# A four-layer token-mixing backbone on one core: two-tensor additions, copies and scale-and-add forms change engines, and the order inside the three-product matmul

## The chip, the cores and the metric

One NeuronCore of one Trainium2 chip runs the whole program in one launch. The metric is the device time in microseconds (us) from the first to the last instruction of one execution, as the runtime reports it, and the median over runs. The engines are called PE (TensorE, the matrix engine), DVE (VectorE), ACT (ScalarE), POOL (GpSimd) and SP (SyncE, which issues the DMAs here).

## The reference, cut to what matters

Four layers work on 512 tokens (256 context, then 256 latent) of width 1024. Each layer has a token mixer and a SwiGLU channel mixer, both with adaLN modulation and RMS norms before and after.

```python
hg, rw, gt = split(modulate(rms_norm(x)) @ w_in)  # 2560 + 1920 + 2048 columns
o_hg = hgrn2_branch(hg)    # 4 heads, both directions: gated linear recurrence, S = diag(f) S + k v^T
o_rw = rwkv7_branch(rw)    # 8 heads, both directions: S = S diag(w) + (S a) b^T + v k^T, o = S r
m = sigmoid(gt_a) * (o_hg @ proj_a) + sigmoid(gt_b) * (o_rw @ proj_b)
x = x + gate * rms_norm(m @ w_out)
x = x + gate * rms_norm((silu(h @ w1a) * (h @ w1b)) @ w2)  # hidden width 2816
```

The first three layers carry context and latent tokens through everything. In the last layer only the latent tokens are needed after the recurrences.

## The kernel before, in words

Activations lie with channels on the partitions and the 512 tokens along the free axis. All large products are done in three parts: a weight tile is loaded as float32 (`wr`, 256 KB: four blocks of 128x128), ACT rounds it to `wh` (fp32r), and a subtraction writes the remainder `wl = wr - wh`; the activations are split likewise into `hh` and `hl`. `mm3` (lines 494 to 497) then accumulates three matmuls per 128x128 block into one PSUM tile `p_ps`. `proj` (line 521) makes one 128-row output of such a product from `load_split` (line 477) and `mm3`. There are four raw buffers and three each for `wh` and `wl`. Which engine makes `wl` is set by `LO` (line 62): DVE in the mixers, POOL in the rest of the first three layers, either in the rest of the last layer.

A layer (line 744) has two stages. **The mixer** runs these streams, which the program lists at line 1312 and which overlap freely:

- `rw_pair` (line 812), four times: prepares two RWKV heads (projections, decays, `kd` at line 888, masked score products `SC`, copies into `SC` at line 951).
- `rw_solve` (line 985), four times: a triangular solve on DVE, 30 steps of two dependent small operations (`S<-XS`, `XS<-XS,S` in the trace), then small matmuls.
- `rw_chain` (line 1031), four times: eight chunk steps, each a handful of 64x64 matmuls (`c_ps`), ACT copies, POOL's `S0P = S * pcs` and DVE's updates of `UV` and `S`; at the end the group norm with its scale and shift at line 1130.
- `hg_head` (line 1140), four times: projections, then seven levels. A level exponentiates the cumulated sums `HA` and `HB` on ACT into `X` and `Y` (`hX` and `hY` in the trace), multiplies `X` by `q` on DVE, makes scores on PE, and doubles the sums' reach with one addition into `HB` and one into `HA` (lines 1232 to 1234, on POOL).
- `gate_tiles` (line 1300): the sixteen gate projections, which nothing in the mixer waits for.

**The rest of a layer** (from line 1343 on) is `proj_a`, `proj_b`, `w_out`, the norms and the channel mixer, with the modulation vectors of the next layer made on DVE beside it.

No queue order is written by hand. Every operation is recorded as a node (`Plan.add`, line 150) with a cost in ns (`Plan.cost`, line 198), and a list scheduler (line 243) puts the nodes of each engine into one fixed order before the program is emitted; nodes recorded through `plan.any` go to DVE or POOL, whichever the plan has free first. Each engine then runs its own list in order and waits on semaphores. The lines of the cost function that bear on the edits are these (`n` is elements per partition; the last three are POOL's, of which the very last serves two-tensor operations and copies):

```python
if eng == "act":
    return (51.0 if psum else 93.0) + n * 0.833 + 93.0 * bool(ptr)
if eng == "vec":
    two = name in ("tensor_scalar", "tensor_copy") and not psum
    return 67.0 + n * (0.53 if two else 1.042) + 61.0 * ptr
...
if name == "tensor_scalar":
    if ptr:
        return 686.0
...
return 150.0 + 2.1 * n
```

Because every instruction is emitted from one place, all carry line 343 in the trace; the tiles tell them apart. In the trace `X8a` holds `TA` (so `kd` is `X8a<-X8a,vv,der`), `X4c` holds `TC`, `BK` the split of a sum's input in `psum2` (line 503), and `nacc<-SS` is the copy at line 1231.

Of the kernel before, what the change touches and what calls it, by code (L numbers as in the profile page):

```python
# [9 lines left out]
F32 = mybir.dt.float32  # L10
F32R = mybir.dt.float32r
U8 = mybir.dt.uint8
AF = mybir.ActivationFunctionType
ALU = mybir.AluOpType
# [15 lines left out]
C = 64  # L30
# [323 lines left out]
def body(ctx, tc, xT, cc, ada_w, w_in, rw_lo, rw_g2, proj_a, proj_b, w_out, ffn_w1, ffn_w2,  # L354
         vecs, lbl, c_id, c_bo, c_sc, c_hg, c_sh, out, depth=4):
    nc = tc.nc
    plan = Plan(nc, tc)
# [134 lines left out]
        return hi, lo  # L492

    def mm3(ps, wh, wl, xh, xl, first, last):
        pe.matmul(ps, wh, xh, start=first, stop=False)
        pe.matmul(ps, wh, xl, start=False, stop=False)
        pe.matmul(ps, wl, xh, start=False, stop=last)

    def split_to(hi, lo, src):
        act.activation(hi, src, AF.Copy)  # L500
# [2 lines left out]
    def psum2(w, src, hi, lo, rg=slice(0, T), tag="s"):  # L503

        act.activation(hi[:, rg], src[:, rg], AF.Copy)
        plan.any.tensor_tensor(out=lo[:, rg], in0=src[:, rg], in1=hi[:, rg].bitcast(F32), op=ALU.subtract)
        ps = sps(tag)
        pe.matmul(ps[:, rg], w, hi[:, rg], start=True, stop=False)
        pe.matmul(ps[:, rg], w, lo[:, rg], start=False, stop=True)
        return ps  # L510
# [233 lines left out]
    def layer(l, pm, xs, xd, hh, hl):  # L744
        last = l == depth - 1
# [5 lines left out]
        def v1(base, i):  # L751
            return vv[:, base + i:base + i + 1]
# [24 lines left out]
        def stacked(src, tags):  # L777

            xs = [st(t, [P, T], F32R) for t in tags]
            for d, x in enumerate(xs):  # L780
                h, o = hd[d], hd[1 - d]
                act.activation(x[h], src[h], AF.Copy)
                plan.any.tensor_tensor(out=x[o], in0=src[h], in1=x[h].bitcast(F32), op=ALU.subtract)
            return xs

        wd = shifted(rwt(12), 12, lmu, 0, "vt")
# [25 lines left out]
        def rw_pair(p):  # L812
# [29 lines left out]
            pool.tensor_scalar(out=sq, in0=sq, scalar1=2.0 ** -40, scalar2=None, op0=ALU.max)  # L842
            act.activation(sq2, sq2, AF.Ln)
            act.activation(sq, sq, AF.Ln)
            pool.tensor_tensor(out=sq, in0=sq, in1=sq2, op=ALU.add)
            act.activation(sq, sq, AF.Exp, scale=-0.5)
            nkk = TC[:, 0, :]
            vec.scalar_tensor_tensor(out=nkk, in0=k, scalar=der[:, p:p + 1], in1=sq, op0=ALU.mult, op1=ALU.mult)
# [6 lines left out]
            share[p] = (ARt, pcs)  # L855
            lws = [t.rearrange("p (x c) -> p x c", x=4) for t in parts()]
            act.activation(lws[0], lw, AF.Copy)
            plan.any.tensor_tensor(out=lws[1], in0=lw, in1=lws[0].bitcast(F32), op=ALU.subtract)
            KD, BKs = [], []

            def lora(x, d, xs):
# [5 lines left out]
            for d in range(2):  # L867
                rv = rev if d else sec
                rv4 = rev4 if d else fwd4
                psw = lora(0, d, wd)  # L870
                sw = TA[:, 0, :]
                sigm(sec(sw), rv(psw), der[:, 12 + d * 4 + p:13 + d * 4 + p], sw)
                yield 2
                psa_ = lora(1, d, ad)
                if d:
                    TD = st("BK", [P, 2, T])
                a = TA[:, 1, :]
                sigm(sec(a), rv(psa_), der[:, 20 + d * 4 + p:21 + d * 4 + p], a)
                yield 3
                cs = TC[:, 1, :]  # L880
                vec.tensor_tensor_scan(out=cs, data0=rmk, data1=sw, initial=0.0, op0=ALU.mult, op1=ALU.add)
                pool.memset(ep[:, :, 0:1], 1.0)
                csc = cs.rearrange("p (c j) -> p c j", j=C)
                act.activation(ep[:, :, 1:], csc, AF.Exp, scale=-EC)
                ip = sw
                act.activation(ip, cs, AF.Exp, scale=EC)
                kd = TA[:, 2 + d, :]
                vec.tensor_scalar(out=kd, in0=a, scalar1=v1(V_KA, p), scalar2=der[:, 4 + p:5 + p], op0=ALU.mult,
                                  op1=ALU.add)
                vec.tensor_tensor(out=sec(kd), in0=sec(kd), in1=rv(k), op=ALU.mult)  # L890
                vec.scalar_tensor_tensor(out=sec(a), in0=sec(a), scalar=-1.0, in1=rv(nkk), op0=ALU.mult,
                                         op1=ALU.mult)
                ipc = ip.rearrange("p (c j) -> p c j", j=C)
                yield 3
                BK = (TD if d else TB[:, 0:2, :]).rearrange("p a (b x j) -> p (a b) x j", x=2, j=C)
                BKs.append(BK)
                for h in range(2):
                    for x, src in ((h, a), (1 - h, kd)):
                        vec.tensor_tensor(out=BK[hd[h], :, x, :], in0=src[hd[h]].rearrange("p (c j) -> p c j", j=C),
                                          in1=ipc[hd[h]], op=ALU.mult)  # L900
                ar = ARt[:, d]
                vec.tensor_tensor(out=ch4(ar[:, :, 0, :]), in0=rv4(nkk), in1=ch4(ep[:, :, 0:C]), op=ALU.mult)
                if last:
                    rr = r[:, 256:512].rearrange("p (c j) -> p c j", j=C)
                    if d:
                        rr = rr[:, ::-1, ::-1]
                    vec.tensor_tensor(out=ar[:, 4:8, 1, :], in0=rr, in1=ep[:, 4:8, 1:], op=ALU.mult)
                else:
                    vec.tensor_tensor(out=ch4(ar[:, :, 1, :]), in0=rv4(r), in1=ch4(ep[:, :, 1:]), op=ALU.mult)
                pool.tensor_copy(pcs[:, d, :], ep[:, :, C])  # L910
                KD.append(kd)
                yield 4
            z0 = hd[p % 2]
# [15 lines left out]
            for s4 in range(0, NCH, 4):  # L929
                yield lambda s4=s4: p == 0 or flags.get(("chain", p - 1), -1) >= s4 + 3  # L930
                yield ("at", par["ps"][p] + par["pn"])
                ss = slice(s4, s4 + 4)
                for h in range(0 if s4 else 2):
                    pool.memset(UV[hd[h], :, 0, h, :], 0.0)
                w = C if last and s4 == 0 else P
                for d in range(2):
                    BK, ar = BKs[d], ARt[:, d]
                    pz = [sps().rearrange("p (s c) -> p s c", s=4) for _ in range(2)]
                    with plan.together(0.55):
                        for i in range(4):  # L940
                            for h in range(2):
                                pe.matmul(pz[h][:, i, 0:w], BK[hd[h], s4 + i, :, :], ar[hd[h], s4 + i, 0:w // C, :],
                                          start=True, stop=True)
                    for h in range(2):
                        hs, psv = hd[h], pz[h]
                        vec.tensor_tensor(out=SC[:, d, ss, h, 0:w], in0=psv[:, :, 0:w],
                                          in1=scm[:, 0:w].unsqueeze(1).to_broadcast([P, 4, w]), op=ALU.mult)
                        if not EA[last]:
                            vec.tensor_tensor(out=ZA[z0, d, ss, h, :], in0=psv[hs, :, 0:C],
                                              in1=scm[hs, 0:C].unsqueeze(1).to_broadcast([C, 4, C]), op=ALU.mult)  # L950
                        pool.tensor_copy(SC[hs, d, ss, h, 0:C], ar[hs, ss, 0, :])
                        yield 1
                    ps = sps()
                    for i in range(4):
                        pe.transpose(ps[:, i * P:(i + 1) * P], BK[:, s4 + i, :, :], ident)
                    act.activation(BKT[:, d, ss, :], ps.rearrange("p (a c) -> p a c", a=4), AF.Copy)
                    yield 1
                    ps = sps()
                    for i in range(2):
                        o0 = (s4 + 2 * i) * C  # L960
                        pe.transpose(ps[:, i * P:(i + 1) * P], (vr if d else v)[:, o0:o0 + P], ident)
                    for g in range(2):
                        pv = ps[hd[g], 0:2 * P].rearrange("p (a h c) -> p a h c", a=2, h=2)
                        for h in range(2):
                            act.activation(UV[hd[1 - h], d, s4 + g:s4 + 4:2, h, :], pv[:, :, h, :], AF.Copy)
                    yield 1
# [64 lines left out]
        def rw_chain(p):  # L1031
# [12 lines left out]
            for s in range(NCH):  # L1044
# [54 lines left out]
                with plan.together(0.75):  # L1099
                    for x in steps:  # L1100
                        st_, i, d, n = x
                        for h in range(2):
# [3 lines left out]
                            else:  # L1106
# [20 lines left out]
            rs = rstd_of(ps, t0, 1.0 / C, GN_EPS, sq)  # L1127
            yield 3
            vec.tensor_tensor(out=y[:, rg], in0=y[:, rg], in1=rs[:, rg], op=ALU.mult)
            vec.tensor_scalar(out=y[:, rg], in0=y[:, rg], scalar1=v1(V_GG, p), scalar2=v1(V_GB, p), op0=ALU.mult,  # L1130
                              op1=ALU.add)
            vec.tensor_tensor(out=y[:, rg], in0=y[:, rg], in1=bv[:, rg], op=ALU.add)
            ps = sps()
# [6 lines left out]
        def hg_head(e):  # L1140
# [67 lines left out]
            for lev in range(7):  # L1208
# [19 lines left out]
                    vec.copy_predicated(AC[:, c0:4, :], hgm[:, lev, :].unsqueeze(1).to_broadcast([P, 4 - c0, C]), ps)  # L1228
                if lev == 5:
                    for g in range(2):  # L1230
                        pool.tensor_copy(AT[hd[g], c0:4, hd[g]], AC[hd[g], c0:4, :])
                for t, o, two in ((HB, T + 2 * h - 1, 1 - T - 2 * h), (HA, h, T - 1)):
                    r = both(t, 0, T + h)
                    pool.tensor_tensor(out=r, in0=r, in1=both(HA, o, two, 0), op=ALU.add)
                yield par["hl"]

            qf, qb = X, Y
# [287 lines left out]
```

## Time and profile before

| what | value |
|---|---|
| median of 3 runs | 4339.58 us (4329.52 to 4346.08) |
| the profiled execution's own time | 4335.38 us |
| its span, first to last instruction | 4333.6 us |
| granted PE clock, mean over the span | 0.925 of full speed |
| busy PE / DVE / ACT / POOL | 3898.9 / 3248.5 / 2147.8 / 1901.6 us |
| PE matmuls | 26290 |

A row of a group reads: line, engine, operation, what it writes <- reads, shapes, count | busy us, mean ns of one | idle time of the engine just before, and what ended most of it. Busy time of PE is modelled and matmuls overlap, so the mean of one is longer than the distance between two. The chain of waits follows the work that ended last back in time; in this trace it reaches from 1482 us to the end.

### The profile page before, as it was taken

To read this page: it belongs to the slowest core of one execution; us is meant where nothing else is said; L and a number is where in the kernel's file an instruction comes from. 1 tells how busy PE (TensorE), PEld (TensorE's weight loads), DVE (VectorE), ACT (ScalarE), POOL (GpSimd) and SP (SyncE) were. 2 spreads that over 40 slices of the span, in tenths; PEclk is the share of its full clock that TensorE was granted. 3 is DMA by queue.
4 is the path that set the end of the run, shared out by engine and by line. 5 is a ranking of instruction groups with operands and counts; after the bars stand their busy time and mean duration, and the time that the engine had idled before them with its cause. 6 is when DMAs were issued, how large, how long until landed. Compare 5 with 4: busy or idle time off the path is not lost.

```text
span 4333.6 us, 71689 instructions
## 1 busy us (share of the span) xinstructions
PE 3898.9 (90%) x26290; PEld 3081.4 (71%) x26290; DVE 3248.5 (75%) x5759; ACT 2147.8 (50%) x4234; POOL 1901.6 (44%) x1622
## 2 busy tenths in 40 slices
PE   7898898799988988999998889899899987888898
PEld 4666666677776666778777767667777875676898
DVE  5988978977479899675536998987854289888665
ACT  4555653433255556534433556554444254566564
POOL 1343543456533435464553243444555433345332
PEclk8999899999998998999999989889999997798999
DMA  4211137455422111363444111116444331111555
GB/s 149 64 53 46 54 100 219 137 167 157 132 87 62 53 49 51 122 210 100 134 121 136 55 47 55 50 45 216 134 134 129 103 113 43 44 56 52 172 151 161
DMA packets 661409, 451.03 MB, mean 104 GB/s; under 512 B 28224, under 2 KB 584256, under 8 KB 661056
## 3 DMA queue, kind: packets, MB, share of 16 engines
q1 hardware_dynamic: 661056, 446.44, 34.6%
q8 instruction: 207, 3.39, 0.3%
q14 instruction: 146, 1.20, 0.1%
HBM read 416.98 MB, written 29.36 MB: 103 GB/s over the span
## 4 chain that ended last, share of the span: by engine, by line
PE 40%; DVE 18%; issue 3%; ACT 2%; DMA 1%; POOL 1%; DVEq 0%; SPq 0%; POOLq 0%; ACTq 0%
PE p_ps L343 31%; PE s_ps L343 4%; DVE XS L343 3%; PE c_ps L343 3%; PE g_ps L343 2%; DVE wl L343 2%; DVE S L343 2%; DVE AR L343 1%; DVE hX L343 1%; DVE UV L343 1%; DVE X8b L343 1%; DVE X8a L343 1%; DVE fn L343 1%; DVE y L343 1%; DVE og L343 1%
## 5 line engine op out<-in xcount | busy, mean ns | idle before, releaser
L343 PE MATMUL p_ps<-hh,wl 128*128 128x512 f32 (+1 forms) x2784 | 1057.9, 397 | 64.6 <-DVE wl L343 48.7
L343 PE MATMUL p_ps<-hh,wh 128*128 128x512 f32 (+1 forms) x2784 | 1062.5, 393 | 35.7 <-ACT wh L343 24.4
L343 PE MATMUL p_ps<-hl,wh 128*128 128x512 f32 (+1 forms) x2784 | 1055.4, 390 | 0.0
L343 ACT ACTIVATE wh<-wr 128x512 fp32r<-128x512 f32 x986 | 608.4, 621 | 812.7 <-PE p_ps L343 726.6
L343 POOL TENSOR_TENSOR wl<-wr,wh 128x512 fp32r<-128x512 f32 x492 | 673.2, 1371 | 696.5 <-ACT wh L343 501.9
L343 PEld LDWEIGHTS p_ps<-hh,wl 128*128 128x128 f32 x2784 | 539.1, 196 | 198.5 <-DVE wl L343 68.3
L343 PEld LDWEIGHTS p_ps<-hh,wh 128*128 128x128 f32 x2784 | 538.3, 196 | 144.3 <-ACT wh L343 37.0
L343 PEld LDWEIGHTS p_ps<-hl,wh 128*128 128x128 f32 x2784 | 538.9, 196 | 93.1 <-issue 6.2
L343 DVE TENSOR_TENSOR wl<-wr,wh 128x512 fp32r<-128x512 f32 (+1 forms) x494 | 364.8, 743 | 126.0 <-ACT wh L343 80.8
L343 POOL TENSOR_SCALAR fn<-fn 128x512 f32<-128x512 f32 (+1 forms) x152 | 230.9, 1519 | 249.3 <-ACT fn L343 232.2
L343 DVE TENSOR_TENSOR fn<-fn,p_ps 128x512 f32<-128x512 f32 (+1 forms) x208 | 127.4, 615 | 254.8 <-ACT fn L343 152.8
L343 POOL TENSOR_SCALAR S0P<-S,pcs 128x64 f32<-128x64 f32 x192 | 148.4, 791 | 345.1 <-DVE S L343 329.8
L343 ACT ACTIVATE fn<-fn 128x512 f32<-128x512 f32 (+1 forms) x304 | 174.4, 574 | 104.6 <-POOL fn L343 100.3
L343 POOL COPY SC<-XS 64x256 f32<-64x256 f32 x128 | 73.6, 575 | 327.7 <-DVE SC L343 321.9
L343 DVE TENSOR_TENSOR XS<-XS,S 64x30 f32<-64x30 f32 (+14 forms) x480 | 208.2, 434 | 11.3
L343 POOL TENSOR_TENSOR HB<-HB,HA 128x512 f32<-128x512 f32 x112 | 162.6, 1452 | 113.9 <-ACT hY L343 110.6
L343 DVE TENSOR_TENSOR S<-XS 64x30 f32<-64x30 f32 (+14 forms) x480 | 198.7, 414 | 11.1
L343 POOL TENSOR_TENSOR HA<-HA 128x512 f32<-128x512 f32 x112 | 144.4, 1289 | 19.7 <-ACT hX L343 14.0
L343 PE MATMUL p_ps<-SC,wh 128*128 128x512 f32 (+1 forms) x440 | 145.6, 367 | 6.4 <-ACT SC L343 4.3
L343 DVE SCALAR_TENSOR_TENSOR UV<-c_ps,pcs,S0P 64x64 f32<-64x64 f32 x384 | 108.6, 283 | 40.6 <-PE c_ps L343 31.1
L343 ACT ACTIVATE fn<-p_ps 128x512 f32<-128x512 f32 (+1 forms) x217 | 113.1, 521 | 50.9 <-PE p_ps L343 33.8
L343 POOL TENSOR_SCALAR X8a<-X8a 128x512 f32<-128x512 f32 x64 | 106.9, 1670 | 41.2 <-ACT X8a L343 38.7
(477 smaller groups left out, 8781.8 us busy)
## 6 DMA issues: line engine op xcount, KB each, us to landing
wr<-ffn_w SPq DMA_DIRECT2D x512, 256.0 KB, 3.0
wr<-w_in SPq DMA_DIRECT2D x408, 256.0 KB, 2.9
hq<-ada_w SPq DMA_DIRECT2D x242, 256.0 KB, 2.9
PB<-ada_w SPq DMA_DIRECT2D x110, 256.0 KB, 2.9
wr<-w_out SPq DMA_DIRECT2D x64, 256.0 KB, 3.3
gts<-fn SPq DMA_DIRECT2D x48, 256.0 KB, 3.1
wr<-proj_a SPq DMA_DIRECT2D x32, 256.0 KB, 3.7
wr<-proj_b SPq DMA_DIRECT2D x32, 256.0 KB, 4.2
```

Source lines behind the costliest of these rows:

```text
L343: getattr(self.eng[self.on[i]], name)(*args, **kw)
```

## The change

`mm3` multiplies by the weights' remainder `wl` first instead of last. Four subtractions and additions that were open to DVE or POOL, or were on POOL, are put on DVE (`psum2`, `stacked`, the sum of two logarithms in `rw_pair`, the split of the low-rank weights), and so are the two additions of each level in `hg_head`. Three kinds of POOL copies go to ACT. Two operations of the form x * scalar + scalar with two per-partition scalars go from DVE to POOL. Nothing of what is computed changes but the order of a sum.

```diff
     def mm3(ps, wh, wl, xh, xl, first, last):
-        pe.matmul(ps, wh, xh, start=first, stop=False)
-        pe.matmul(ps, wh, xl, start=False, stop=False)
-        pe.matmul(ps, wl, xh, start=False, stop=last)
+        pe.matmul(ps, wl, xh, start=first, stop=False)
+        pe.matmul(ps, wh, xh, start=False, stop=False)
+        pe.matmul(ps, wh, xl, start=False, stop=last)
@@ psum2 @@
-        plan.any.tensor_tensor(out=lo[:, rg], in0=src[:, rg], in1=hi[:, rg].bitcast(F32), op=ALU.subtract)
+        vec.tensor_tensor(out=lo[:, rg], in0=src[:, rg], in1=hi[:, rg].bitcast(F32), op=ALU.subtract)
@@ stacked @@
-                plan.any.tensor_tensor(out=x[o], in0=src[h], in1=x[h].bitcast(F32), op=ALU.subtract)
+                vec.tensor_tensor(out=x[o], in0=src[h], in1=x[h].bitcast(F32), op=ALU.subtract)
@@ rw_pair @@
-            pool.tensor_tensor(out=sq, in0=sq, in1=sq2, op=ALU.add)
+            vec.tensor_tensor(out=sq, in0=sq, in1=sq2, op=ALU.add)
...
-            plan.any.tensor_tensor(out=lws[1], in0=lw, in1=lws[0].bitcast(F32), op=ALU.subtract)
+            vec.tensor_tensor(out=lws[1], in0=lw, in1=lws[0].bitcast(F32), op=ALU.subtract)
...
-                vec.tensor_scalar(out=kd, in0=a, scalar1=v1(V_KA, p), scalar2=der[:, 4 + p:5 + p], op0=ALU.mult,
+                pool.tensor_scalar(out=kd, in0=a, scalar1=v1(V_KA, p), scalar2=der[:, 4 + p:5 + p], op0=ALU.mult,
                                   op1=ALU.add)
...
-                pool.tensor_copy(pcs[:, d, :], ep[:, :, C])
+                act.activation(pcs[:, d, :], ep[:, :, C], AF.Copy)
...
-                        pool.tensor_copy(SC[hs, d, ss, h, 0:C], ar[hs, ss, 0, :])
+                        act.activation(SC[hs, d, ss, h, 0:C], ar[hs, ss, 0, :], AF.Copy)
@@ rw_chain @@
-            vec.tensor_scalar(out=y[:, rg], in0=y[:, rg], scalar1=v1(V_GG, p), scalar2=v1(V_GB, p), op0=ALU.mult,
+            pool.tensor_scalar(out=y[:, rg], in0=y[:, rg], scalar1=v1(V_GG, p), scalar2=v1(V_GB, p), op0=ALU.mult,
                               op1=ALU.add)
@@ hg_head @@
-                        pool.tensor_copy(AT[hd[g], c0:4, hd[g]], AC[hd[g], c0:4, :])
+                        act.activation(AT[hd[g], c0:4, hd[g]], AC[hd[g], c0:4, :], AF.Copy)
                 for t, o, two in ((HB, T + 2 * h - 1, 1 - T - 2 * h), (HA, h, T - 1)):
                     r = both(t, 0, T + h)
-                    pool.tensor_tensor(out=r, in0=r, in1=both(HA, o, two, 0), op=ALU.add)
+                    vec.tensor_tensor(out=r, in0=r, in1=both(HA, o, two, 0), op=ALU.add)
```

## Rows read from the trace of the kernel before

**Rows 1.** The page, part 1: busy time of each engine over the span.

```profile
PE 3898.9 (90%) x26290; PEld 3081.4 (71%) x26290; DVE 3248.5 (75%) x5759; ACT 2147.8 (50%) x4234; POOL 1901.6 (44%) x1622
```

**Rows 2.** Busy time by stretch, mixers: length; PE, PEld, DVE, ACT, POOL; clock.

```profile
87.00:670.00 583.00, 529.03 (x4272) 391.23 (x4271) 504.49 (x957) 338.49 (x678) 247.76 (x233) 0.92 0.24 71
...
3544.00:4057.00 513.00, 436.80 (x3723) 348.89 (x3722) 444.19 (x907) 299.95 (x655) 212.90 (x220) 0.84 0.21 61
sum 2274.00, PE 2025.53 PEld 1531.60 DVE 1956.81 ACT 1315.49 POOL 947.78; mean PE 506.38 PEld 382.90 DVE 489.20 ACT 328.87 POOL 236.95
```

**Rows 3.** Busy time by stretch, the four rests of layers: sum.

```profile
sum 1972.00, PE 1815.03 PEld 1510.31 DVE 1253.45 ACT 797.94 POOL 945.19; mean PE 453.76 PEld 377.58 DVE 313.36 ACT 199.48 POOL 236.30
```

**Rows 4.** The chain of waits, 2403 to 2996 us (third mixer), by line.

```profile
by line: PE p_ps L343 28.9%; PE s_ps L343 10.6%; PE c_ps L343 7.9%; DVE XS L343 7.2%; PE g_ps L343 5.3%; issue 5.2%; DVE wl L343 4.7%; DVE S L343 4.1%; DVE X8b L343 2.7%; DVE AR L343 2.7%; DVE hX L343 2.5%; DVE X8a L343 2.0%; DVE UV L343 1.
```

**Rows 5.** Groups of POOL's instructions, shapes kept apart: what leaves POOL.

```profile
L343 POOL TENSOR_TENSOR HB<-HB,HA 128x512 f32<-128x512 f32 x112 | 162.6, 1452 | 113.9 <-ACT hY L343 110.6
L343 POOL TENSOR_TENSOR HA<-HA 128x512 f32<-128x512 f32 x112 | 144.4, 1289 | 19.7 <-ACT hX L343 14.0
...
L343 POOL COPY SC<-XS 64x256 f32<-64x256 f32 x128 | 73.6, 575 | 327.7 <-DVE SC L343 321.9 <-DVE S L343 2.0 <-PE g_ps L343 1.9
...
L343 POOL TENSOR_TENSOR X4c<-X4c,X8a 128x512 f32<-128x512 f32 x16 | 22.6, 1415 | 14.7 <-ACT X4c L343 14.4
...
L343 POOL TENSOR_TENSOR BK<-X4c,BK 128x512 fp32r<-128x512 f32 x11 | 14.4, 1308 | 58.9 <-ACT BK L343 56.5 <-DMA wr<-w_in 2.4
```

**Rows 6.** Groups of DVE's instructions, shapes kept apart.

```profile
L343 DVE TENSOR_TENSOR wl<-wr,wh 128x512 fp32r<-128x512 f32 x486 | 361.9, 749 | 125.1 <-ACT wh L343 79.8 <-PE p_ps L343 25.9 <-ACT y L343 9.1
...
L343 DVE TENSOR_TENSOR hX<-hX,hq 128x512 f32<-128x512 f32 x128 | 105.3, 823 | 10.5 <-ACT hX L343 9.0
...
L343 DVE TENSOR_TENSOR SC<-s_ps,scm 128x512 f32<-128x512 f32 x112 | 76.5, 684 | 7.3 <-PE s_ps L343 5.5 <-PE c_ps L343 0.2
...
L343 DVE TENSOR_TENSOR X8b<-X8a 64x512 f32<-64x512 f32 x64 | 54.2, 847 | 4.1 <-ACT X8a L343 2.8
...
L343 DVE TENSOR_SCALAR X8a<-X8a,vv,der 128x512 f32<-128x512 f32 x32 | 27.6, 861 | 2.9 <-ACT X8a L343 1.6 <-issue 1.2
...
L343 DVE TENSOR_TENSOR fn<-fn,p_ps 128x256 f32<-128x256 f32 x52 | 21.6, 417 | 16.3 <-ACT fn L343 15.2 <-PE p_ps L343 1.0
```

**Rows 7.** Groups of DVE's instructions, shapes taken together: the solve's two operations.

```profile
L343 DVE TENSOR_TENSOR XS<-XS,S 64x30 f32<-64x30 f32 (+14 forms) x480 | 208.2, 434 | 11.3
L343 DVE TENSOR_TENSOR S<-XS 64x30 f32<-64x30 f32 (+14 forms) x480 | 198.7, 414 | 11.1
```

**Rows 8.** Timeline, first mixer, from 202.9 us: start, us, engine.

```profile
203.27 1.70 POOL L343 TENSOR_TENSOR HA<-HA 128x512 f32<-128x512 f32 x1 [0.82 <-ACT hX L343]
...
204.06 1.46 DVE L343 TENSOR_TENSOR X8a<-X8a,X8b 128x512 f32<-128x512 f32 x1
```

**Rows 9.** Timeline of the first mixer from 209.5 us on.

```profile
209.92 1.69 POOL L343 TENSOR_SCALAR fn<-fn 128x512 f32<-128x512 f32 x1
...
210.18 1.09 DVE L343 TENSOR_TENSOR wl<-wr,wh 128x512 fp32r<-128x512 f32 x1
```

**Rows 10.** Timeline of POOL, first mixer: 2x - 1 at line 791.

```profile
85.01 0.84 POOL L343 TENSOR_SCALAR vt<-vt 128x512 f32<-128x512 f32 x1
```

**Rows 11.** Groups of ACT's instructions, shapes kept apart: 256 elements.

```profile
L343 ACT ACTIVATE fn<-XS 128x256 f32<-128x256 f32 x120 | 47.9, 414 | 61.2 <-DVE XS L343 20.6 <-PE s_ps L343 19.1 <-DMA XS<-xT 16.6
```

**Rows 12.** Who PE waited for: us in total, times, longest us.

```profile
PE p_ps L343 <- DVE wl L343: 49.9, 40, 5.3
PE c_ps L343 <- DVE S L343: 45.6, 39, 3.9
PE p_ps L343 <- ACT wh L343: 29.5, 30, 3.2
...
PE p_ps L343 <- POOL wl L343: 19.3, 27, 1.9
```

**Rows 13.** The chain of waits, a dense stretch: start, length, matmuls.

```profile
2233.24 76.53 PE p_ps L343 x330
```

## The prediction

> **What bounds it now.** I read the page first: PE is busy for 90% of the span and DVE for 75% [rows 1]. A mean over such different stages says little, so I split the span. In the four mixers, 2274 us together, PE is busy for 2026 us and DVE for 1957, 89% and 86%, with ACT at 58% and POOL at 42%; the granted PE clock lies between 0.84 and 0.92 there [rows 2]. In the rests of the layers, 1972 us, PE is at 92% and DVE at 64% [rows 3]. All edits but the order within `mm3` touch the mixers alone, so the question is what DVE and PE do there. The chain of waits through the third mixer is mostly PE, in all its tiles, with DVE's solve, `wl`, level product and RWKV preparation between (XS, S, AR, wl, hX, X8a, X8b and UV add up to some 27%); POOL and ACT are in no named piece [rows 4]. So neither emptying POOL nor loading ACT pays or costs directly. What counts is DVE's time, and how often PE waits for it.
>
> **POOL's two-tensor additions also cost DVE time.** DVE's product of an SBUF tensor with a PSUM one takes 684 ns for 512 elements, and the same count with both inputs in SBUF takes 823 (level product), 847 (RWKV preparation) and 749 (`wl`) on the mean [rows 6]. The timeline shows why: POOL's addition runs from 203.27 to 204.97, and a DVE addition that began at 204.06 takes 1.46 us [rows 8]. The excess over all such DVE work in the mixers: level product 128 x 139 ns = 18 us; preparation 64 x 163 = 10; `wl` 486 x 65 = 32. The solve's 960 operations take 424 ns on the mean [rows 7]; their sizes are (31 - i) x i for i = 1 to 30, 165 elements on the mean, and the line through 417 ns at 256 and 684 at 512 [rows 6] gives 322 there, so 960 x 102 = 98 us. Together 158 us.
>
> **The change, term by term.** The profiled execution took 4335.4 us, 4.2 us (0.1%) under the median of the runs, and the sum starts from it.
>
> 1. *Additions to DVE.* 224 in the levels and 16 sums of logarithms, plus 27 remainders of `psum2` that the plan had put on POOL (11 in the row, two more groups of 10 and 6) [rows 5], 267 in all. On DVE each costs 0.684 us [rows 6]: +183 us. What they held up before is bounded by nothing and by their whole POOL time, 162.6 + 144.4 + 22.6 + about 36 = 366 us [rows 5]. I take the excess just found, 160 us, 0.60 us per addition: it is nearest, since it was measured on the DVE operations themselves. `stacked` and the low-rank split are on DVE already, but for single ones.
> 2. *Scale-and-add to POOL.* 32 `kd` leave DVE at 861 ns each [rows 6], 28 us; the 16 of the group norm are shorter for the last layer, about 10 us. On POOL each takes between 0.84 us (the same two operations with constants [rows 10]) and 1.7 us (a one-input minimum [rows 9]); two scalar pointers put it above the lower end, and I take 1.1. That is 0.25 us more on the way to `BK`, 48 x 0.25 = 12 us of latency. They hold DVE too, but less than an addition: beside the 1.69 us minimum a `wl` took 1.09 us, 0.41 over the 0.68 of an undisturbed operation [rows 6, 9]. Not each meets one; 48 x 0.41 = 20 us at most.
> 3. DVE's sum is +183 - 160 - 38 = -15 us of 1957, and up to 20 back. **DVE's load hardly changes.** The chain holds 27% of 593 us, 160 us, out of DVE's about 505 in that mixer: a third. So -15 us is worth -5, and kd's latency and hold (12 + 20) about +8.
> 4. *The levels.* One goes from 1452 + 1289 on POOL to 2 x 684 on DVE, 1.37 us less, 112 times: 153 us of latency. The heads' pieces in the chain are g_ps and hX, 7.8% [rows 4], and no POOL addition is in it, so the additions are mostly hidden: 8% of 153, -12.
> 5. *Copies to ACT.* 128 into `SC`, 32 at line 1231 and 32 tiny ones cost ACT at most 192 x 0.414 = 80 us [rows 11], on an engine that is 58% busy; its cover is that PE and DVE are later. Between 0 and 80 x 5% if a few come in front of the chain's copies: +4. POOL's own one-input work (`S0P`, the minima) no longer queues behind additions: -5.
> 6. *The order against reality.* The plan is made with 67 + 1.042 ns per element, 600 ns for 512, on DVE. Before, an operation planned at 600 could take 1.46 us [rows 8], and every engine's fixed order was late against it. PE waited 50 us for `wl` on DVE and 46 us for the chain's state update [rows 12], 96 us, with many smaller waits beside. Afterwards DVE's work is in the plan as such, and its durations are nearer to their cost. I take a quarter of these 96 us: -25, an estimate between 0 and 96.
> 7. *`wl` first.* PE could begin a block of twelve matmuls with `wh` alone, and met `wl` two matmuls later. In a dense stretch a matmul comes every 76.53 / 330 = 0.23 us [rows 13], so a late `wl` now costs up to 0.46 us more. There were 40 + 27 waits for `wl`, and 30 for `wh` that become waits for `wl` (0.75 us later on DVE) [rows 12]: 67 x 0.46 + 30 x 0.75 = 53 us at most. The plan knows of the wait and can put other matmuls before it, so +10. In return `hl` is wanted one matmul later, worth nothing that a row shows.
>
> Sum: -5 + 8 - 12 + 4 - 5 - 25 + 10 = -25, so 4310 us; against the median of the runs it is 0.7% less, against the profiled execution 0.6%. A second limit keeps it small: the gate projections fill PE up to the mixer's end, and PE's work is the same.
>
> **Rivals.** (a) *No change.* The excess of DVE was worth just what the additions cost, the plan's shape changes by chance, and one-input POOL operations hold DVE like additions. For it: PE's 89%. By it items 4 and 6 vanish, and -5 + 8 + 4 - 5 + 10 = +12 is left, 4347. The Trainium skill ("SBUF — State Buffer", Who interferes with whom) says that the port pair which DVE and GpSimd share goes to the first of them for its whole instruction, and that a DVE instruction with two SBUF inputs contends with any GpSimd instruction that reads SBUF. By that rule `kd` and the group norm would hold DVE for all of their 1.1 us, 48 x 1.1 = 53 us instead of 20, a third of the difference, +11, on the chain, and 4358. The row speaks against the rule for one-input work: `wl` was done 0.34 us before the minimum ended [rows 9].
>
> (b) *Slower: DVE waits for ACT.* An engine runs in order. POOL stood idle for 110.6 us before the additions into `HB` until ACT had read `hY`, and 14 us before those into `HA` [rows 5], which cost nothing there. On DVE the same wait holds up everything queued behind: the solves, `wl`, the chain's updates. All of it is 125 us of DVE; with what hangs on `wl` first and a third to a half on the chain, 4335 + 50 + 15 = 4400. It decides once more than a third of these waits stay. Against it: the level product, which waits for the same kind of ACT result on DVE, had 9.0 us of it in 128 [rows 6], so the plan places DVE's work well.
>
> (c) *More than forecast.* If all of the 96 us goes and the solves, 98 us of excess, are in the chain whole while the additions lie beside PE: 4335 - 96 - 20 = 4220.
>
> **How the numbers follow.** About 0.5% is what a measurement of this kernel can tell from no change. The forecast has 0.40, on its own 4290 to 4325, which is mostly faster by over 0.5%; (a) 0.25; (b) 0.27; (c) 0.08. From the forecast 0.05 falls within 0.5%. So faster 0.43, same 0.30, slower 0.27. The range reaches from (c) nearly to the end of (b): 4225 to 4390, which leaves out the far tails of both.
>
> **What would show it.** Right: the level product near 690 ns and the solve's pair near 330; DVE's busy time in the mixers within 2% of 1957 us; POOL's down by 400; waits of PE for the chain's state update and `XS` shorter. Wrong: `HB` or `HA` on DVE with tens of us of idle time ended by ACT (rival b); PE's waits for `wl` past 100 us (item 7); `kd` on POOL over 2 us; DVE's operations as long as before although POOL adds no more, which would undo item 1.

## The result, and the profile after

The changed kernel takes 4371.62 us in the median (4356.97 to 4379.33), the kernel before beside it on the same chip 4344.89. The ratio is 1.0054 with a 95% interval of 1.0038 to 1.0070: slower, by about as much as the bound of 0.5%. Forecast was 4310, faster. The profiled execution took 4373.45 us, its span is 4371.3.

The page of the changed kernel, part 1 (busy time and share of the span):

```profile
PE 3890.0 (89%) x26290; PEld 3083.2 (71%) x26290; DVE 3297.0 (75%) x5982; ACT 2214.1 (51%) x4426; POOL 1481.9 (34%) x1207
```

Against [rows 1], PE does the same 26290 matmuls, POOL is 420 us emptier, ACT 66 us fuller and DVE 49 us fuller.

Busy time by stretch, the four mixers of the changed kernel (length; PE, PEld, DVE, ACT, POOL; clock, share of the DMA engines, GB/s):

```profile
87.00:717.00 630.00, 542.20 (x4292) 405.88 (x4292) 521.26 (x1049) 356.77 (x730) 138.43 (x127) 0.88 0.24 73
1293.00:1875.00 582.00, 518.86 (x4240) 386.41 (x4239) 499.15 (x1018) 356.22 (x729) 132.24 (x126) 0.91 0.23 70
2427.00:3032.00 605.00, 534.49 (x4296) 403.11 (x4295) 507.70 (x1029) 357.41 (x732) 149.49 (x131) 0.90 0.23 70
3575.00:4103.00 528.00, 438.17 (x3753) 349.25 (x3753) 450.35 (x966) 320.00 (x709) 115.36 (x123) 0.84 0.21 61
sum 2345.00, PE 2033.72 PEld 1544.64 DVE 1978.46 ACT 1390.39 POOL 535.52; mean PE 508.43 PEld 386.16 DVE 494.62 ACT 347.60 POOL 133.88
```

And the rests of the layers:

```profile
sum 1939.00, PE 1798.39 PEld 1500.54 DVE 1279.65 ACT 790.45 POOL 940.10; mean PE 449.60 PEld 375.14 DVE 319.91 ACT 197.61 POOL 235.03
```

The mixers grew from 2274 to 2345 us and the rests shrank from 1972 to 1939 [rows 2, 3]. The mixer's DVE time is only 22 us above that of before, 1%. PE, however, was idle for 2345 - 2034 = 311 us of the mixers where it had been idle for 2274 - 2026 = 248. The first mixer alone is 47 us longer, at a granted clock of 0.88 instead of 0.92.

Whom PE waited for over the whole span (us, times, longest):

```profile
PE p_ps L343 <- DVE wl L343: 85.2, 48, 12.5
PE s_ps L343 <- DVE XS L343: 83.0, 26, 10.0
PE p_ps L343 <- POOL wl L343: 58.5, 53, 3.7
PE c_ps L343 <- DVE S L343: 28.2, 23, 3.5
```

In the kernel before, beside [rows 12]:

```profile
PE s_ps L343 <- DVE XS L343: 35.4, 23, 3.4
...
PE g_ps L343 <- DVE hX L343: 20.7, 16, 3.6
```

Against these, the wait for the chain's state update fell from 45.6 to 28.2 us and the wait for `wh` is gone; the waits for `wl` rose from 49.9 + 19.3 to 85.2 + 58.5, and the one for `XS` from 35.4 to 83.0.

### The profile page after: what moved, and what is told of

Its sections match the earlier page's. It is cut to its first block, busy times and chain, and to the rows that moved or that the text cites. A ratio compares the mean times of both kernels' runs of the same rounds, so it can differ in the third digit from the quotient of the medians.

```text
span 4371.3 us, 71264 instructions
## 1 busy us (share of the span) xinstructions
PE 3890.0 (89%) x26290; PEld 3083.2 (71%) x26290; DVE 3297.0 (75%) x5982; ACT 2214.1 (51%) x4426; POOL 1481.9 (34%) x1207
## 4 chain that ended last, share of the span: by engine, by line
PE 34%; DVE 11%; issue 7%; POOL 4%; ACT 2%; DMA 1%; POOLq 0%; SPq 0%; DVEq 0%; ACTq 0%
PE p_ps L343 26%; PE s_ps L343 4%; POOL wl L343 3%; PE c_ps L343 2%; PE g_ps L343 2%; DVE XS L343 2%; DVE wl L343 1%; DVE X8b L343 1%; DVE AR L343 1%; DVE S L343 1%; DVE X8a L343 0%; DVE X4c L343 0%; DVE BK L343 0%; DVE UV L343 0%; DMA wr<-ffn_w 0%
## 5 line engine op out<-in xcount | busy, mean ns | idle before, releaser
L343 PE MATMUL p_ps<-hh,wl 128*128 128x512 f32 (+1 forms) x2784 | 1096.4, 399 | 134.9 <-DVE wl L343 82.4
L343 DVE TENSOR_TENSOR wl<-wr,wh 128x512 fp32r<-128x512 f32 (+1 forms) x498 | 346.8, 701 | 113.9 <-ACT wh L343 108.9
L343 ACT ACTIVATE fn<-fn 128x512 f32<-128x512 f32 (+1 forms) x304 | 174.9, 576 | 112.4 <-POOL fn L343 107.7
L343 DVE TENSOR_TENSOR S<-XS 64x30 f32<-64x30 f32 (+14 forms) x480 | 160.9, 335 | 11.3
L343 DVE TENSOR_TENSOR XS<-XS,S 64x30 f32<-64x30 f32 (+14 forms) x480 | 158.1, 329 | 11.1
L343 PE MATMUL s_ps<-XS,BK 64*64 64x64 f32 (+2 forms) x1024 | 80.9, 304 | 65.5 <-DVE XS L343 58.5
L343 PEld LDWEIGHTS s_ps<-XS,BK 64*128 64x128 f32 (+1 forms) x1024 | 68.8, 206 | 83.2 <-issue 60.9
L343 PEld LDWEIGHTS c_ps<-UV,SC 128*64 128x64 f32 x1024 | 75.6, 148 | 61.8 <-issue 46.8
```

The costliest lines, as they stand in the source:

```text
L343: getattr(self.eng[self.on[i]], name)(*args, **kw)
```

## What the operations cost now

Groups of DVE's instructions, shapes kept apart (busy us, mean ns of one | idle before, and what ended it):

```profile
L343 DVE TENSOR_TENSOR wl<-wr,wh 128x512 fp32r<-128x512 f32 x490 | 343.6, 706 | 112.0 <-ACT wh L343 107.0 <-issue 0.7
L343 DVE TENSOR_TENSOR hX<-hX,hq 128x512 f32<-128x512 f32 x128 | 88.4, 691 | 11.2 <-ACT hX L343 9.6
L343 DVE TENSOR_TENSOR HA<-HA 128x512 f32<-128x512 f32 x112 | 85.9, 767 | 0.6
L343 DVE TENSOR_TENSOR HB<-HB,HA 128x512 f32<-128x512 f32 x112 | 84.1, 751 | 15.2 <-ACT hY L343 14.7
...
L343 DVE TENSOR_TENSOR X8b<-X8a 64x512 f32<-64x512 f32 x64 | 44.6, 698 | 1.6 <-ACT X8a L343 0.7
```

The solve's two operations, shapes taken together:

```profile
L343 DVE TENSOR_TENSOR S<-XS 64x30 f32<-64x30 f32 (+14 forms) x480 | 160.9, 335 | 11.3
L343 DVE TENSOR_TENSOR XS<-XS,S 64x30 f32<-64x30 f32 (+14 forms) x480 | 158.1, 329 | 11.1
```

What came to POOL:

```profile
L343 POOL TENSOR_SCALAR X8a<-X8a,vv,der 128x512 f32<-128x512 f32 x32 | 28.2, 882 | 13.3 <-ACT X8a L343 10.9 <-POOL UV L343 0.9
...
L343 POOL TENSOR_SCALAR y<-y,vv 128x512 f32<-128x512 f32 x12 | 12.1, 1009 | 185.1 <-DVE y L343 185.1
```

So the excess that POOL's additions had put on DVE is gone as forecast: the level product fell from 823 to 691 ns, the preparation from 847 to 698, the solve from 434 and 414 to 329 and 335 [rows 6, 7]. Rival (b) had wanted tens of us of idle time before `HB` and `HA`, and there are some 15. Nothing in these rows tells why the kernel is slower.

## The experiments

The theories that the expectations name are these. **A**: the order within `mm3` costs by itself. **B**: the moves between engines cost by themselves. **C**: it is the chance of the planned order, since every edit makes the list scheduler write new queues. **D**: the two halves work against each other. **E**: the plan costs DVE's operations too low. **F**: the changed kernel's plans are slower as a class. **G**: it is the two together, `wl` first where DVE makes `wl` and the moves have filled DVE's list; it says how D and F come about.

### One half of the change at a time

```diff
-        pe.matmul(ps, wh, xh, start=first, stop=False)
+        pe.matmul(ps, wl, xh, start=first, stop=False)
...
```

> The kernel before with the new order in mm3 alone (weights' remainder first), all engines as before. Theory A (the order costs: PE meets the remainder before it can start a block, and its waits for wl grew from 69 us to 144 us): 15 to 45 us over the kernel before, with PE's waits for wl over 100 us. Theory B (the moves between engines cost: DVE's fixed order runs later and PE waits for the products XS, 35 us before and 83 us after): within 10 us of the kernel before. Theory C (any change of the plan shuffles the order, and the time moves by chance): anything within 30 us either way, with no growth of one kind of wait.

Measured: the order alone 4315.58 us, ratio 0.9943 [0.9931, 0.9955]. The rest of the change with the old order:

```diff
-        pe.matmul(ps, wl, xh, start=first, stop=False)
-        pe.matmul(ps, wh, xh, start=False, stop=False)
-        pe.matmul(ps, wh, xl, start=False, stop=last)
+        pe.matmul(ps, wh, xh, start=first, stop=False)
+        pe.matmul(ps, wh, xl, start=False, stop=False)
+        pe.matmul(ps, wl, xh, start=False, stop=last)
```

> All moves between engines with the old order in mm3. Theory A: within 10 us of the kernel before, or faster by up to 30 us as I forecast for the moves alone. Theory B: 20 to 40 us over the kernel before, with PE's waits for XS near 80 us as in the changed kernel. Theory C: anything within 30 us either way.

Measured: 4331.98 us, 0.9982 [0.9969, 0.9995]. Each half by itself is not slower, and the whole is. As far as one plan of each can tell, A and B fall as theories of a cost that either half carries alone. The levels alone, of all the moves, on the kernel before:

```diff
-                    pool.tensor_tensor(out=r, in0=r, in1=both(HA, o, two, 0), op=ALU.add)
+                    vec.tensor_tensor(out=r, in0=r, in1=both(HA, o, two, 0), op=ALU.add)
```

> The kernel before with only the two additions of each level (HB and HA, 224 in all) on DVE. My forecast's main item: DVE's busy time in the mixers unchanged within 2%, the solve's operations near 330 ns, and 0 to 25 us faster than before. Theory B, in the form that DVE is late with more instructions in its order: 10 to 30 us slower. Theory C: anything within 30 us.

Measured: 4337.07 us, 0.9994 [0.9982, 1.0006], no change. Yet PE's waits for `XS` are already 78.6 us in it, more than twice those of before. With the order alone, where DVE's work is what it was, they are 60.3 us, in a faster plan. So that wait does not come from the levels alone, and it is not by itself the price.

### How much is the chance of the plan

An edit to none of the operations, which shifts the plan a little: one constant of the cost function by 1 ns. The orders are made anew, and a few of the operations that are open to DVE or POOL change sides (DVE has 5759 before and 5754 with the first of these edits).

```diff
-            return 67.0 + n * (0.53 if two else 1.042) + 61.0 * ptr
+            return 68.0 + n * (0.53 if two else 1.042) + 61.0 * ptr
```

> The kernel before with nothing moved: only the plan's constant for a DVE instruction goes from 67 to 68 ns, so the fixed orders are made anew. Theories A and B: within 10 us of the kernel before. Theory C: it moves by 10 us or more, and that is the size that any edit moves by chance.

> The changed kernel with the same idle edit as the null run (67 to 68 ns in the plan's cost of a DVE instruction). Theory C (the 25 to 30 us that the changed kernel is slower than its two halves are chance of one order): it moves by 10 us or more, most likely down, to 4330 to 4360. Theory D (the two halves work against each other: with wl first and DVE fuller, PE waits for wl at the head of a block): it stays within 10 us of 4371, and PE's waits for wl stay above 120 us.

Measured: on the kernel before 4350.85 us, 1.0026 [1.0014, 1.0039]; on the changed kernel 4344.48, 0.9996 [0.9986, 1.0007]. The same with ACT's constant:

```diff
-            return (51.0 if psum else 93.0) + n * 0.833 + 93.0 * bool(ptr)
+            return (51.0 if psum else 94.0) + n * 0.833 + 93.0 * bool(ptr)
```

> The changed kernel with another idle edit (93 to 94 ns in the plan's cost of an ACT instruction). Theory C: 4320 to 4365, and different from the other idle edit by 10 us or so. Theory D: within 10 us of 4371, PE's waits for wl above 120 us.

> The kernel before with the second idle edit (93 to 94 ns for an ACT instruction). Theory C (chance of the fixed order, the same for all four arms: before, order alone, moves alone, both): 4320 to 4370, as the three plans of the changed kernel spread from 4344 to 4390. Theory F (the changed kernel's plans are slower as a class): it stays under 4355.

Measured: on the changed kernel 4389.6 us, 1.0095 [1.0078, 1.0112]; on the kernel before 4318.06, 0.9944 [0.9927, 0.9960]. Such idle edits thus moved the kernel before over 0.8% and the changed kernel over 1.0%, which is more than the difference in question. Of one plan against one plan nothing follows here. From this point on a half of the change is a class of several plans, with the same two idle edits made in each.

> The order in mm3 alone with the first idle edit. Theory C: the 24 us that the order alone gained are chance, and it comes out between 4325 and 4365. Theory F with a gain of the order: under 4325 again.

> The order in mm3 alone with the second idle edit. Theory C: between 4325 and 4365, and 10 us or more from the other idle edit or from 4316. Theory F with a gain of the order: under 4325.

> The moves alone with the first idle edit. Theory C: between 4320 and 4370. Theory F, with a loss that comes only where both halves meet: 4320 to 4340 like the first plan of the moves. In both, the streams up to the last output of the heads end earlier than before (2176 us in the four mixers against 2232), and PE's waits for XS are over 60 us.

> The moves alone with the second idle edit, the third plan of that arm. Theory G: 4300 to 4345, as the other two plans of the moves (4332 and 4323), with PE's waits for weights at 92 to 102 us and for XS over 60. Theory C: could as well be 4360.

Measured, order alone: 4353.42 us, 1.0027 [1.0017, 1.0037], and 4317.32, 0.9942 [0.9926, 0.9959]. Moves alone: 4323.41, 0.9953 [0.9937, 0.9969], and 4321.89, 0.9949 [0.9935, 0.9963]. The means of three plans each are 0.9990 (before), 0.9971 (order), 0.9961 (moves) and 1.0048 (both). The classes overlap but for one pair: all three plans of the moves are below all three of both. That is still few plans, and C stood.

### The plan's cost of DVE's operations

```diff
-            return 67.0 + n * (0.53 if two else 1.042) + 61.0 * ptr
+            return 150.0 + n * (0.53 if two else 1.042) + 61.0 * ptr
```

> The changed kernel with the plan's fixed cost of a DVE instruction at 150 ns, which is what the rows give (417 ns at 256 elements, 684 at 512), instead of 67. Theory E (PE stands idle in the mixers because its fixed order counts on DVE earlier than DVE comes, and more DVE instructions make that worse): PE's waits for XS and wl, 83 and 144 us, fall by a third or more, PE's idle time in the mixers from 312 us to under 270, and the time to 4310 to 4350. Theories C and D: no such fall of the waits; the time anywhere within 20 us of 4371.

> The kernel before with the same 150 ns in the plan. Theory E: it gains as well, but less than the changed kernel, 0 to 20 us, since what holds DVE up there (POOL's additions) is in no cost. Theory C: anything within 20 us either way.

Measured: 4463.21 us, 1.0269 [1.0253, 1.0286], on the changed kernel and 4405.45, 1.0141 [1.0125, 1.0157], on the kernel before. E falls. A constant that agrees better with the measured durations made a worse order: PE's waits for `XS` in these two plans,

```profile
PE s_ps L343 <- DVE XS L343: 116.5, 24, 14.8
```

on the changed kernel and

```profile
PE s_ps L343 <- DVE XS L343: 165.6, 28, 12.8
```

on the kernel before. Why is open.

### Where the order matters

`mm3` serves two places: the mixers, where DVE makes `wl`, and the rests of the layers, where POOL makes it in the first three. A field of the program that is zero inside the mixers and not in the rests tells them apart. All moves, and `wl` first in the rests only:

```diff
+        for w, x, p in (((wl, xh, 0), (wh, xh, 1), (wh, xl, 2)) if ada["rate"] else ((wh, xh, 0), (wh, xl, 1), (wl, xh, 2))):
+            pe.matmul(ps, w, x, start=first and p == 0, stop=last and p == 2)
```

> All moves, with wl first only outside the mixers (proj_a to the channel mixer) and the old order inside them. Theory G (the loss is made in the mixers, where wl first makes a block wait for a subtraction that the fuller DVE delivers late): the mixers fall from 2338 us, the mean of three plans with both, to about 2290, PE's waits for wl on DVE from 76 to 92 us to under 50, and the time to 4310 to 4345. Theory C (chance): the time anywhere from 4320 to 4390.

> As the run with wl first outside the mixers alone, with the idle edit of ACT's cost (94 ns), the plan that gave 4390 with both. Theory G: 4310 to 4345 again. Theory C: no nearer to that than to 4370.

and, with `if not ada["rate"]`, in the mixers only:

> All moves, with wl first only inside the mixers. Theory G: the mixers stay at 2310 us or more, PE's waits for wl on DVE stay over 70 us, and the time is 4350 to 4390; PE's waits for wl on POOL go back from about 60 to about 20 us. Theory C: anywhere from 4320 to 4390.

> As the run with wl first inside the mixers alone, with the idle edit of ACT's cost. Theory G: 4350 to 4395. Theory C: no nearer to that than to 4330.

Measured. In the rests only: 4318.04 us, 0.9946 [0.9931, 0.9962], and with ACT's idle edit 4300.03, 0.9908 [0.9892, 0.9924], under the 4310 to 4345 that theory G gave for it. In the mixers only: 4374.83, 1.0078 [1.0059, 1.0096], and with the idle edit 4362.11, 1.0051 [1.0036, 1.0067]. The loss comes with the order inside the mixers. Last, the engines of before with `wl` first in the mixers only:

> The engines of the kernel before, with wl first inside the mixers alone. Theory G in full (the loss needs both: the order, and a DVE that the moves have filled): 4320 to 4350, PE's waits for wl on DVE 37 to 68 us as in the three plans with the order alone, not the 76 to 92 us with both. If the order inside the mixers costs by itself, whatever the engines: 4355 to 4380 and waits for wl on DVE over 75 us.

Measured: 4337.47 us, 0.9989 [0.9980, 0.9998]. In this plan the order in the mixers costs nothing without the moves.

The classes side by side. The mixers' lengths are taken from the busy time by stretch (first of the layer's `wd` to its last gate write), and PE's idle and busy time in the first three, the mean over the plans, from the same rows. The fourth mixer does not tell the last two lines apart (525 to 537 and 526 to 533 us).

| class | plans | ratio to before | first three mixers, us | PE idle / busy in them, us | PE's wait for DVE's `wl`, us |
|---|---|---|---|---|---|
| engines of before, `wl` last in the mixers | 3 | 0.9944 to 1.0026 | 1742 to 1773 | 177 / 1581 | 42.9 to 50.4 |
| engines of before, `wl` first in the mixers | 4 | 0.9942 to 1.0027 | 1754 to 1785 | 196 / 1569 | 36.7 to 67.7 |
| moves, `wl` last in the mixers | 5 | 0.9908 to 0.9982 | 1749 to 1760 | 182 / 1571 | 21.7 to 39.1 |
| moves, `wl` first in the mixers | 5 | 0.9996 to 1.0095 | 1778 to 1828 | 214 / 1598 | 75.4 to 91.1 |

With the engines of before, the two orders can't be told apart. With the moves, all five plans of the one class are faster than all five of the other. If order had no effect there, ten plans would fall apart so cleanly in one of 252 ways of dealing them out; that counts them as independent, which plans that differ by an idle edit need not be. So the loss needs both, the order in the mixers and the moves. This much of G is shown, and C is true of every single plan, and not of the classes.

That the moves do it by filling DVE's list is not shown. DVE does not make `wl` later: in the first three mixers, worked out from the traces, it begins `wl` on the mean 3.5 to 3.8 us after ACT has written `wh` in the five plans with both, 3.2 to 3.7 us with the order alone, and 4.2 to 5.4 us with `wl` last. The moves also gave 192 copies to ACT, which makes `wh`, and no run takes the two apart.

The waits of PE in one plan of each of the last two classes. The moves alone (e2_moves):

```profile
PE s_ps L343 <- DVE XS L343: 85.1, 20, 13.5
PE p_ps L343 <- ACT wh L343: 41.1, 44, 3.0
PE p_ps L343 <- DVE wl L343: 29.1, 25, 6.7
...
PE p_ps L343 <- POOL wl L343: 19.8, 30, 1.9
```

The moves and `wl` first in the mixers (e17_mix_order):

```profile
PE s_ps L343 <- DVE XS L343: 83.7, 25, 9.9
PE p_ps L343 <- DVE wl L343: 80.2, 48, 12.2
...
PE p_ps L343 <- POOL wl L343: 17.9, 32, 1.9
...
PE p_ps L343 <- ACT wh L343: 12.7, 15, 1.4
```

The wait for `XS` is the same in both, so it does not make the difference. The wait for `wl` on DVE does differ, by 51 us, and the wait for `wh` falls from 41.1 to 12.7, so the two together grow by 23 us. The fastest plan of all (e18_rest_order2) shows the other side:

```profile
PE s_ps L343 <- DVE XS L343: 92.4, 26, 8.3
PE p_ps L343 <- POOL wl L343: 63.0, 57, 4.0
...
PE p_ps L343 <- DVE wl L343: 25.6, 28, 4.7
```

Its waits for POOL's `wl` are as long as those of the changed kernel, 63 us, and it is the fastest. A sum of waits is a place to look, not a price: in the rests the order added some 40 us of waits for POOL's `wl`, at no loss.

Where the 60 us of the first three mixers are (1753 in the mean with the moves, 1812 with both): busy time by stretch of e18_rest_order2,

```profile
86.00:672.00 586.00, 524.15 (x4292) 392.81 (x4291) 509.22 (x1029) 357.88 (x731) 142.25 (x128) 0.91 0.24 75
1251.00:1832.00 581.00, 522.00 (x4281) 389.83 (x4280) 509.52 (x1029) 356.68 (x730) 143.88 (x128) 0.91 0.24 75
2374.00:2956.00 582.00, 511.39 (x4283) 384.73 (x4282) 508.55 (x1030) 357.91 (x732) 143.37 (x128) 0.92 0.24 75
```

PE is busy for 1558 of 1749 us, idle for 191; in the changed kernel's rows above it is busy for 1596 of 1817, idle for 221. DVE's busy time is the same, 1527 and 1528. So 30 us of these 68 are idle time of PE, and in the other 38 it is busy longer for the same matmuls, at granted clocks of 0.88, 0.91 and 0.90 against 0.91, 0.91 and 0.92.

The means of the classes in the table say the same, 32 us of idle time and 27 us of longer busy time, and something more. With the engines of before `wl` first costs PE idle time too, 19 us, but PE is busy for 12 us less beside it. So what sets the two pairs of classes apart is mostly PE's busy time for the same matmuls, and the granted clock of these stretches goes with it: its means are 0.913 and 0.914 with the engines of before, 0.907 and 0.897 with the moves. Why it falls in the one pair and not in the other is not shown.

One of the waits, near the end of the changed kernel's first mixer. Timeline from 662.4 us (start, us, engine, what [idle before, and what ended it]):

```profile
662.44 0.39 PE L343 MATMUL p_ps<-hl,wh 128*128 128x512 f32 x1
664.31 2.19 ACT L343 ACTIVATE UV<-SC 128x512 fp32r<-128x512 f32 x4 [4.44 <-DMA SC<-od]
...
666.41 1.13 ACT L343 ACTIVATE wh<-wr 128x512 fp32r<-128x512 f32 x2
667.39 0.74 DVE L343 SCALAR_TENSOR_TENSOR vt<-hq,cvec,vt 128x512 f32<-128x512 f32 x1
...
671.41 0.74 DVE L343 SCALAR_TENSOR_TENSOR og<-PB,cvec,og 128x512 f32<-128x512 f32 x1
...
672.07 1.28 DVE L343 TENSOR_TENSOR wl<-wr,wh 128x512 fp32r<-128x512 f32 x2
...
672.81 0.80 PE L343 MATMUL p_ps<-hh,wl 128*128 128x512 f32 x1 [9.98 <-DVE wl L343]
```

PE's list stands before a block that begins with `wl`. ACT had been held by a DMA for 4.4 us before it made `wh`; `wh` was there at 667.5; DVE then had the modulation vectors, 667.39 to 672.1, ahead of `wl` in its list. From 667.5 on PE lacked nothing but DVE's `wl`, 5.3 us. With the old order and the same lists it could have had two matmuls of this block behind it by then, 0.46 us at the distance of [rows 13]. So the order does not cost the 5.3 us by itself here; it costs through what the plan puts where. What the whole idle stretch did to the clock, by stretch (length; PE; ...; clock behind POOL's count):

```profile
650.00:662.80 12.80, 12.36 (x54) 9.57 (x52) 7.89 (x15) 5.76 (x11) 3.18 (x2) 1.00 0.90 281
662.80:672.80 10.00, 0.03 (x1) 0.00 (x0) 7.83 (x12) 6.37 (x12) 3.64 (x2) 0.63 0.86 295
672.80:675.00 2.20, 2.19 (x5) 1.81 (x6) 1.86 (x4) 2.20 (x5) 0.00 (x0) 0.50 0.88 246
675.00:677.00 2.00, 2.00 (x9) 1.54 (x8) 2.00 (x4) 0.22 (x1) 0.00 (x0) 0.83 0.99 325
677.00:680.00 3.00, 3.00 (x15) 2.47 (x14) 3.00 (x6) 0.63 (x1) 0.00 (x0) 1.00 0.78 233
```

After the idle stretch PE ran at the lower of its two levels, 1.2 GHz (the row with 0.50), and started five matmuls in 2.2 us, where at 0.23 us each [rows 13] there would be nine or ten; with the row behind it, at 0.83, some 1.4 us more was lost that way, an estimate from the shares in these rows.

Not settled: why PE waits longer in all before such blocks when the moves and the order meet. The 12.5 us wait of the changed kernel, 83 us into its fourth mixer, recurs at that place in all five plans of its class (longest waits 12.2 to 12.6 us) and the fourth mixer is no longer for it than with the moves alone; the loss in the first three is made of many waits. No single move was tried together with `wl` first, the levels neither, so which of them it takes is open.

## Why the prediction was wrong

It forecast 4310 and the kernel took 4371.62, inside the range of 4225 to 4390 but on the side that had 0.27. That it lies inside is luck: the upper end was rival (b)'s, and (b)'s wait did not come. The 62 us are made up of the runs' own level (4344.89 beside it against the 4335.4 that the sum started from, 9.5), of items 1 to 6, which were worth -17 instead of -35 (moves alone, mean of three plans 0.9961; 18), and of item 7, which was worth about +38 instead of +10 (mean of both, 1.0048, less 0.9961; 28); the rest, some 6 us, is this one plan and the spread of its runs.

- **Items 1 and 3, DVE's load, right.** DVE's mixer time was to stay within 2% of 1957 and is 1978. The 160 us of excess went. The additions cost 0.751 and 0.767 instead of 0.684 us, 17 us more in all, most of the 22 by which the load rose: the term was short by that, and by the sum's -15.
- **Item 2, `kd` and the group norm, right.** 0.88 and 1.01 us on POOL against 1.1. The median of `kd` is 0.77, below the lower end of 0.84 that came from a single row. What one-input POOL work still holds of DVE is small: 7 ns on 128 level products, 14 on 64 of the preparation, 22 on 490 `wl`, and 10 on 960 solve steps above the 322 worked out before, some 22 us, beside 536 us of POOL in the mixers. The trace of the kernel before says more, as far as the spans of POOL are exact. Of the `wl` and level products that DVE began at least 0.8 us before the end of a running POOL instruction, all 74 beside a one-input scalar operation ended before it did (median 0.68 us, mean 0.78; alone 0.69), and of 41 beside a two-tensor addition only 10 did (mean 1.37 us). The Trainium skill ("SBUF — State Buffer", Who interferes with whom) calls the ports that DVE and GpSimd share an exclusive lock, which two SBUF inputs on DVE and a GpSimd read contend for; as the prediction read it, `kd` and the norm alone could have held DVE for all their 44 us. These traces don't agree with a hold of the whole instruction by one-input work.
- **Items 4 and 5, hardly felt, right in kind.** The levels alone gave 0.9994. The copies into `SC` took 413 ns each on ACT, and no wait for one of them is among PE's nine longest sums.
- **Item 6, the waits fall, wrong.** A quarter of 96 us was to go. The wait for the state update fell (45.6 to 28.2), the one for the level product also (20.7 to 5.3), but the one for `XS` rose from 35.4 to 83.0. It rose with the levels alone as well, in all four plans with the order alone (52.5 to 85.4) and in all plans with the moves (60.4 to 92.4). The prediction counted the waits that the moves would shorten and none that a new plan would lengthen. A fuller list of DVE is not the whole reason, since the order alone leaves DVE's work as it was. The second limit that it named fits: with the moves alone (e2_moves) the last outputs of the streams were stored 2177 us into the four mixers instead of 2232, and the mixers took 2286 us instead of 2274. The fourth mixer took 500 to 522 us in the seven plans with the engines of before and 525 to 537 in all ten with the moves; no item had that, and its cause is open.
- **Item 7, `wl` first, the step that decided.** The bound of 53 us was worked out as two matmuls' worth of delay per late `wl`, in the rests as well, and +10 taken, because "the plan knows of the wait and can put other matmuls before it". The plan did not do so well enough: its queues are fixed beforehand, and PE, in order, stands before the block. In the mixers the order costs 1.0065 - 0.9961 = 1.0%, some 45 us; in the rests it costs nothing (0.9927 against 0.9961 in the mean). That 45 is near the bound is luck: it is made of idle time and of longer busy time at a lower clock, not of two matmuls per `wl`. Moreover the price isn't of the order alone, with the engines of before it is nil. The prediction priced every edit by itself and had no term for two of them together; what makes the two dear together is open.
- **Rivals.** (b), slower, was right in sign and wrong in mechanism: DVE waited 14.7 us for ACT before `HB`, not more than a third of 125. (a), no change, is nearest to what the moves did alone. The sign "PE's waits for `wl` past 100 us" was named as what would show item 7 wrong, and came: 144. It is a poor sign all the same: with the order alone these waits were 112.4 and 128.5 us in two plans that were faster than before (0.9943 and 0.9942).

## What to carry to other kernels

In a kernel whose queues a list scheduler writes, make idle edits first and see how far the time moves: here 0.8%, so only classes of plans can be compared. Two edits that are harmless or good alone can cost together; test each with and without the other, and in each stage where it applies. Here the better version is the changed kernel with `wl` first only outside the mixers: 4318.04 and 4300.03 us in its two plans, both faster than either kernel, the second by 0.92% against before. As a class they have two plans, and the kernel before ran in 4318.06 us too with ACT's idle edit, so of a gain over it no more than the class means say is shown (0.9927 against 0.9990).

## Unexpected of the hardware

The addition into `HB`, always 128x512 elements, has two durations on DVE (min/median/max ns):

```profile
L343 DVE TENSOR_TENSOR HB<-HB,HA x112: 664/683/1165, 177.8 to 4055.2; 128x512 f32<-128x512 f32 x112
```

The long ones are those of the first of the seven levels, where the sum is taken over pieces of one element; the first of the first head and the addition into `HA` behind it, in the timeline:

```profile
177.79 1.15 DVE L343 TENSOR_TENSOR HB<-HB,HA 128x512 f32<-128x512 f32 x1
180.99 1.15 DVE L343 TENSOR_TENSOR HA<-HA 128x512 f32<-128x512 f32 x1
```

POOL has no two-tensor operation near these times any more, so the access to such small pieces is the likeliest cause; it was not tried by itself. It is 0.47 us more, 32 times, and the prediction had taken 0.684 for all levels.
